# MLP steps of a hybrid decoder trunk: the quarter products set in runs of three, two, four and five

## The chip, the cores and the metric

One Trainium2 chip, one core. The metric is the device time of one execution in microseconds; 3 runs of the kernel before gave 1048.12 to 1048.92 with a median of 1048.6. Matrix products run on TensorE (PE), and ScalarE (ACT) and VectorE (DVE) prepare their operands. SyncE (SP) issues plain DMA loads, and GpSimd (POOL) issues loads that add into their destination ("accumulates").

## The reference

Two layers on 512 rows of width 1024 in float32. Layer 0 mixes by latent attention and layer 1 by gated linear attention; behind each mixer stands the MLP that this case is about:

```python
def sq_relu_mlp(xn, w_up, w_down):          # w_up 1024 x 4096, w_down 4096 x 1024
    hid = jnp.square(jax.nn.relu(xn @ w_up))
    return hid @ w_down

for i in range(DEPTH):                      # DEPTH = 2
    x = x + mixer(rms_norm(x, norm_mix[i]))
    x = x + sq_relu_mlp(rms_norm(x, norm_mlp[i]), w_up[i], w_down[i])
return rms_norm(x, final_norm)
```

## The kernel before

Every float32 operand is split into a high part, which is its rounding to the type that TensorE reads, and a low part, which is the remainder. A product is then three matmuls: high by high, high by low, low by high. For a weight piece, `piece` does the split: ACT writes the high part (`wh`, L110) and then DVE the low part (`wl`, L113), 128 x 1024 elements each, into tiles of four buffers each.

The MLP works in eight blocks of 512 hidden units. In step b (0 to 6) it computes the up product of block b+1 and the down product of block b. Each of the two is a 2 x 2 block product done with seven quarter products in place of eight, in the manner of Strassen and Winograd. So a step has seven `up_product`s (24 matmuls each, 256 columns, L958) and seven `down_product`s (12 matmuls each, 512 columns, L967).

The names: `a11` and `a12` are halves of the up tile A1, `s3` and `a22` of the tile A2, and S1 is a third up tile. `d11`, `d12`, `dS1`, `dS3`, `d22` are down tiles. A2, S1, dS1 and dS3 are sums of two quadrants of the weights, which `fetch` makes with a plain load on SP followed by an accumulate on POOL. `q11` to `q22` are the quarters of the hidden block. Some operands are sums formed on DVE inside the step, among them `d11 = dS1 + d11`, `a11 = S1 + a11` and `q11 = q11 + (q22 - q12)` (with its sign turned later). PSUM has four single banks ("u") for up products and two double banks, "d" and "e", for down products. The output totals S11, S12, SU, S21 and S5 lie in SBUF. S21 and S5 go through a bank: copied in, added onto by the product, and copied out.

Buffers carry over between steps: `after(name)`, called where the tile `name` has had its last use, fetches a tile of the next step into the same room. Which one is a table:

```python
NEXT = {"d11": "dS1", "S1": "S1", "d12": "d11", "A1": "A1", "dS3": "d12", "dS1": "dS3", "A2": "A2", "d22": "d22"}
```

Here the next step's dS1 goes into the room of d11, whose last use is in the fifth product of the step.

Each engine executes its own list of instructions in order. A scheduler makes the lists from the program: it may move an instruction of one product among those of another. The queues of SP and POOL are in order too, and an instruction that waits holds what stands behind it.

## Time and profile before

| | |
|---|---|
| median of 3 runs | 1048.6 us |
| the profiled execution's own time | 1048.94 us |
| its span in the profile | 1047.2 us |
| PE busy | 1038.0 us (99%) |
| DVE, ACT busy | 874.3 us (83%), 699.2 us (67%) |
| granted TensorE clock, mean | 0.998 |

The profiled execution is 0.34 us above the median, and 1.74 us of it lie outside the span. The MLP of layer 0 runs from about 207 to 502 us in the span, that of layer 1 from about 745 us to the end. Busy shares are means over the whole program. What the change is worth is decided inside the MLP steps, on the engine that is never idle there.

### The profile page before, as it was taken

The numbers are of one execution on the slowest core, as the hardware profiler recorded it, in microseconds if no ns is written. First come the engines' busy times: TensorE is split into PE (matmuls) and PEld (weight loads), VectorE is DVE, ScalarE is ACT, GpSimd is POOL, SyncE is SP. The second block draws the span as 40 slices with busy tenths as digits, with TensorE's granted clock in tenths as the row PEclk, the third lists the DMA queues.
The fourth block names the chain that finished last, engine by engine and source line by source line (L and its number), as shares of the span: only waits on it lengthen the run. The fifth ranks groups of instructions, "written<-read, shape, count | busy, mean of one in ns | idle before, by whom it ended". The sixth has DMA issues, their size and how long they took to land.

```text
span 1047.2 us, 15642 instructions
## 1 busy us (share of the span) xinstructions
PE 1038.0 (99%) x5966; PEld 905.1 (86%) x5966; DVE 874.3 (83%) x1340; ACT 699.2 (67%) x1074; POOL 114.6 (11%) x128
## 2 busy tenths in 40 slices
PE   9999999999999999999999999999999999999997
PEld 7788888889999999998888888888888999999995
DVE  7889977989899889898687399469789989989993
ACT  7667754567777777776445475565677777777784
POOL 7400010301101111000000000000010111111000
PEclk9999999999999999999999999999999999999999
DMA  7401235776976887843212222164496697697612
GB/s 230 124 21 41 81 94 148 226 184 159 236 189 151 216 210 161 202 161 121 66 66 81 83 79 67 55 161 152 90 253 153 178 236 171 160 237 185 159 61 81
DMA packets 120492, 149.97 MB, mean 143 GB/s; under 512 B 9344, under 2 KB 86144, under 8 KB 120288
## 3 DMA queue, kind: packets, MB, share of 16 engines
q1 hardware_dynamic: 95920, 117.76, 35.3%
q0 software_dynamic: 22400, 29.36, 17.7%
q10 hardware_dynamic: 2096, 1.84, 0.6%
q8 instruction: 47, 0.77, 0.3%
q14 instruction: 29, 0.24, 0.1%
HBM read 144.49 MB, written 4.19 MB: 142 GB/s over the span
## 4 chain that ended last, share of the span: by engine, by line
PE 90%; DVE 4%; ACT 3%; DMA 2%; issue 1%; SPq 0%; ACTq 0%; DVEq 0%
PE ps L967 26%; PE ps L958 25%; PE ps L118 10%; PE ps L120 10%; PE ps L119 10%; PE ps L1174 2%; PE ps L1429 1%; PE ps L135 1%; PE ps L1209 1%; DVE wl L113 1%; DMA wraw<-in_mla_w_in_dram 1%; PE ps L1556 1%; DVE acc L252 0%; ACT wh L110 0%; DMA xT<-in_x_dram 0%
## 5 line engine op out<-in xcount | busy, mean ns | idle before, releaser
L967 PE MATMUL ps<-wh,set 128*128 128x512 f32 x784 | 253.7, 392 | 0.3 <-ACT set L110 0.3
L110 ACT ACTIVATE wh<-wraw 128x1024 fp32r<-128x1024 f32 x139 | 146.6, 1058 | 97.3 <-PE ps L119 42.0
L113 DVE TENSOR_TENSOR wl<-wraw,wh 128x1024 fp32r<-128x1024 f32 x139 | 170.1, 1224 | 42.7 <-ACT wh L110 41.7
L967 PEld LDWEIGHTS ps<-wh,set 128*128 128x128 f32 x784 | 147.0, 188 | 30.2 <-ACT set L110 0.7
L958 PE MATMUL ps<-T,wh 128*128 128x256 f32 x896 | 156.0, 276 | 0.0
L967 PE MATMUL ps<-wl,set 128*128 128x512 f32 x392 | 152.9, 390 | 0.0
L113 DVE TENSOR_TENSOR wl<-comb,wh 128x1024 fp32r<-128x1024 f32 x112 | 136.7, 1221 | 16.4 <-ACT wh L110 16.4
L958 PEld LDWEIGHTS ps<-T,wh 128*128 128x128 f32 x896 | 137.6, 188 | 2.4
L110 ACT ACTIVATE wh<-comb 128x1024 fp32r<-128x1024 f32 x112 | 118.2, 1056 | 23.4 <-PE ps L958 8.5
L958 PE MATMUL ps<-T,wl 128*128 128x256 f32 x448 | 124.0, 277 | 0.0
L958 PE MATMUL ps<-set,wh 128*128 128x256 f32 x672 | 117.7, 277 | 0.0
L118 PE MATMUL ps<-set,wh 128*128 128x512 f32 x280 | 109.8, 392 | 0.0
L119 PE MATMUL ps<-set,wh 128*128 128x512 f32 x280 | 109.8, 392 | 0.0
L120 PE MATMUL ps<-set,wl 128*128 128x512 f32 x280 | 109.6, 391 | 0.0
L958 PEld LDWEIGHTS ps<-set,wh 128*128 128x128 f32 x672 | 103.8, 188 | 2.4
L958 PE MATMUL ps<-set,wl 128*128 128x256 f32 x336 | 93.2, 277 | 0.0
L967 PEld LDWEIGHTS ps<-wl,set 128*128 128x128 f32 x392 | 73.8, 188 | 13.5
L958 PEld LDWEIGHTS ps<-T,wl 128*128 128x128 f32 x448 | 84.1, 188 | 0.1
L947 POOL DMA_DIRECT2D comb<-in_mlp_w_down_dram x28 | 33.5, 1197 | 304.8 <-DMA comb<-in_mlp_w_down_dram 143.6
L958 PEld LDWEIGHTS ps<-set,wl 128*128 128x128 f32 x336 | 63.1, 188 | 0.0
L120 PEld LDWEIGHTS ps<-set,wl 128*128 128x128 f32 x280 | 52.6, 188 | 11.4 <-DVE wl L113 0.4
L119 PEld LDWEIGHTS ps<-set,wh 128*128 128x128 f32 x280 | 52.6, 188 | 11.1 <-DVE set L750 0.2
(396 smaller groups left out, 2027.0 us busy)
## 6 DMA issues: line engine op xcount, KB each, us to landing
comb<-in_mlp_w_down_dram SPq DMA_DIRECT2D x74, 512.0 KB, 4.9
wraw<-in_mlp_w_up_dram SPq DMA_DIRECT2D x32, 1024.0 KB, 8.2
comb<-in_mlp_w_down_dram POOLq DMA_DIRECT2D x28, 512.0 KB, 7.6
wraw<-in_gla_w_in_dram SPq DMA_DIRECT2D x12, 1024.0 KB, 5.2
comb<-in_mlp_w_up_dram SPq DMA_DIRECT2D x14, 512.0 KB, 4.2
comb<-in_mlp_w_up_dram POOLq DMA_DIRECT2D x14, 512.0 KB, 8.7
wraw<-in_mlp_w_up_dram POOLq DMA_DIRECT2D x14, 512.0 KB, 6.2
wraw<-in_mla_w_o_dram SPq DMA_DIRECT2D x4, 1024.0 KB, 4.9
```

Source lines behind the costliest of these rows:

```text
L110: order(ACT.activation(hi, src, AF.Copy))
L113: lo_eng.tensor_tensor(lo, src, f(hi), ALU.subtract)
L118: PE.matmul(psum, wh, xh, start=start, stop=False)
L119: PE.matmul(psum, wh, xl, start=False, stop=False)
L120: PE.matmul(psum, wl, xh, start=False, stop=stop)
L135: PE.transpose(psum, src, ident[: src.shape[0], : src.shape[0]])
L947: POOL.dma_start(t, q(b, *more), accum_op=ALU.add)
L958: PE.matmul(o, a_, x_, start=start and j == 0 and k == 0 and n == 0, stop=k == KH - 1 and n == 2, skip_group_check=True)
L967: PE.matmul(o, x_, w_, start=start and k == 0 and n == 0, stop=k == 1 and n == 2, skip_group_check=True)
L1174: PE.matmul(p, a, x, start=False, stop=k == 3 and n == 2, skip_group_check=True)
L1209: PE.matmul(o, a, b_, start=False, stop=k == 3 and n == 2, skip_group_check=True)
L1429: PE.matmul(p[:, t - t0], k[:, t * P : (t + 1) * P], moving[:, t], start=True, stop=True)
```

## The change

Step 0 of each layer keeps the old function `step`, with its last two products swapped (`down_21` before `up_t4`). Steps 1 to 6 of each layer use a new function, `step_in_runs`. It has the same fourteen products with the same operands, in the order

D(d11) | U(a11) U(S1) U(a11 + S1) | D(d12) D(d11 + dS1) | U(a12) U(s3) U(22) U(a22) | D(d12 + d11) D(dS3) D(dS1) D(d22)

where U is an up and D a down product. The four last downs and the first one of the next step make five in a row. The total S5 goes through two single "u" banks in place of the double bank "e"; S21 now uses "e". The table of rooms changes: the next dS1 goes into the room of d12, whose last use is now the first of the four last downs, right behind the last use of A2.

```diff
-            opening = b == 0 and nxt is not None
+            opening = nxt is not None
...
-            if b == 0:
-                order = up_t2, down_11, up_t1, down_22, up_22, down_12, up_t3
-            else:
-                order = down_11, up_t2, up_t1, down_22, down_12, up_22, up_t3
-            ends = (up_t4, down_21) if b in (0, NB - 2) else (down_21, up_t4)
-            for product in (*order, down_5, *ends):
+            for product in (up_t2, down_11, up_t1, down_22, up_22, down_12, up_t3, down_5, down_21, up_t4):
                 product()
+
+        def step_in_runs(b, q, r, after):
...
+            def onto(total, a, parts):
+                pair = [bank("u"), bank("u")]
+                cols = [total[:, i * 512 : (i + 1) * 512] for i in range(2)]
+                for p, c in zip(pair, cols):
+                    copied(p, c)
+                down_product(pair, a, parts, False)
+                for p, c in zip(pair, cols):
+                    copied(c, p)
+
+            d = two_banks("d")
+            down_product(d, d11, parts_of_quad(q11), True)
+            e = copied(two_banks("e"), d)
+            DVE.tensor_tensor(d11, ds1, d11, ALU.add)
+            DVE.tensor_tensor(q12, q22, q12, ALU.subtract)
+            DVE.tensor_tensor(q11, q11, q12, ALU.add)
+
+            w, w2, z, y = (bank("u") for _ in range(4))
+            up_product(z, a11, "11", True)
+            copied(y, z)
+            DVE.tensor_tensor(a11, s1, a11, ALU.add)
+            up_product(w, s1, "T1", True)
+            copied(w2, w)
+            after("S1")
+            up_product(z, a11, "T2", False)
+            u = copied(tmp(), z)
+
+            down_product(e, d12, parts_of_quad(q21), False)
+            DVE.tensor_tensor(S11, e, S11, ALU.add)
+            DVE.tensor_tensor(q21, q21, q11, ALU.subtract)
+            down_product(d, d11, parts_of_quad(q11, -1.0), False)
+            e = copied(two_banks("e"), d)
...
+            up_product(z, a22, "T4", False)
+            finish(z, 1, 0, r)
+            after("A2")
+
+            down_product(e, d12, parts_of_quad(q22), False)
+            DVE.tensor_tensor(S12, e, S12, ALU.add)
+            after("d12")
...
+            onto(S5, ds1, parts_of_quad(q22, -1.0))
+            after("dS1")
+            e = copied(two_banks("e"), S21)
+            down_product(e, d22, parts_of_quad(q21, -1.0), False)
+            copied(S21, e)
+            after("d22")
...
-        NEXT = {"d11": "dS1", "S1": "S1", "d12": "d11", "A1": "A1", "dS3": "d12", "dS1": "dS3", "A2": "A2", "d22": "d22"}
+        NEXT = {"S1": "d11", "d11": "S1", "d12": "dS1", "dS3": "d12", "dS1": "dS3", "d22": "d22", "A1": "A1", "A2": "A2"}
...
-            step(b, Q[b % 2], Q[(b + 1) % 2], after)
+            (step_in_runs if b else step)(b, Q[b % 2], Q[(b + 1) % 2], after)
```

Three places in the lists of instructions show what the scheduler made of it, all at the turn from step 2 to step 3 of layer 0.

First, the accumulates on POOL. Before, one round in order is dS1 (`comb_3267`), S1 (`comb_3332`, from the up weights), dS3 (`comb_3469`) and A2 (`wraw_3527`), and then the next dS1:

```order
L947 DMA comb_3267<-in_mlp_w_down_dram 128x2x512
L947 DMA comb_3332<-in_mlp_w_up_dram 128x4x256
L947 DMA comb_3469<-in_mlp_w_down_dram 128x2x512
L937 DMA wraw_3527<-in_mlp_w_up_dram 128x4x256
L947 DMA comb_3657<-in_mlp_w_down_dram 128x2x512
```

After, S1 (`comb_3303`), A2 (`wraw_3439`), dS1 (`comb_3461`), dS3 (`comb_3510`), and then the next S1:

```order
L947 DMA comb_3303<-in_mlp_w_up_dram 128x4x256
L937 DMA wraw_3439<-in_mlp_w_up_dram 128x4x256
L947 DMA comb_3461<-in_mlp_w_down_dram 128x2x512
L947 DMA comb_3510<-in_mlp_w_down_dram 128x2x512
L947 DMA comb_3696<-in_mlp_w_up_dram 128x4x256
```

The accumulate of dS1 stood three ahead of that of A2; it now stands directly behind it, and the list of SP likewise has the plain loads of A1, A2 and dS1 one behind the other.

Second, DVE where the sum with dS1 stands. Before (L1013 is `d11 = dS1 + d11`; L1014 and L1015 make q12 and q11; the L113 rows write low parts):

```order
L113 TENSOR_TENSOR wl_3532<-wraw_3411,wh_3531 128x1024
L1063 TENSOR_TENSOR tmp_3443<-ps_3330,tmp_3441 128x512
L1009 TENSOR_TENSOR wraw_3411<-comb_3332,wraw_3411 128x1024
L859 SCALAR_TENSOR_TENSOR tmp_3445<-tmp_3443,rstd_2203 128x512
L113 TENSOR_TENSOR wl_3565<-comb_3354,wh_3564 128x1024
L1014 TENSOR_TENSOR set_2146<-set_2148,set_2146 128x512
L1013 TENSOR_TENSOR comb_3354<-comb_3267,comb_3354 128x1024
L1015 TENSOR_TENSOR set_2145<-set_2145,set_2146 128x512
```

After (L1105 is that sum, L1107 makes q11, L1112 is `a11 = S1 + a11`; `wl_3565` is the low part of a11, `wl_3595` of S1, and the engine's preceding row L1149 adds a finished product to the total SU):

```order
L113 TENSOR_TENSOR wl_3540<-comb_3230,wh_3539 128x1024
L1149 TENSOR_TENSOR xT<-ps_618_3143,xT 128x1024
L1105 TENSOR_TENSOR comb_3230<-comb_3461,comb_3230 128x1024
L1107 TENSOR_TENSOR set_2145<-set_2145,set_2146 128x512
L113 TENSOR_TENSOR wl_3565<-wraw_3406,wh_3564 128x1024
L113 TENSOR_TENSOR wl_3595<-comb_3303,wh_3594 128x1024
L1112 TENSOR_TENSOR wraw_3406<-comb_3303,wraw_3406 128x1024
```

Before, the low part of a11 and the sum a11 + S1 stood ahead of the sum with dS1; now both stand behind it.

Third, ACT and PE right behind that place. ACT after (L844 turns the sign of q11, `sum` is S5, `xT` is S21, `ps_675_3555<-ps_672_3536` copies bank d into bank e, `wh_3625` is the high part of a11 + S1, `wh_3657` that of d12):

```order
L110 ACTIVATE wh_3564<-wraw_3406 128x1024
L1090 ACTIVATE sum_2157<-ps_3488 128x512
L1090 ACTIVATE sum_2157<-ps_3489 128x512
L110 ACTIVATE wh_3594<-comb_3303 128x1024
L844 ACTIVATE set_2155<-set_2145 128x512
L110 ACTIVATE set_2149<-set_2148 128x512
L1090 ACTIVATE xT<-ps_668_3513 128x1024
L110 ACTIVATE wh_3625<-wraw_3406 128x1024
L110 ACTIVATE set_2151<-set_2146 128x512
L1090 ACTIVATE ps_675_3555<-ps_672_3536 128x1024
L110 ACTIVATE wh_3657<-comb_3484 128x1024
```

PE after, at the end of the product with a11 (`wh_3564`) and the start of the one with S1 (`wh_3594`):

```order
L958 MATMUL ps_3562<-set,wh_3564 128x256 x2
L958 MATMUL ps_3562<-set,wl_3565 128x256
L967 MATMUL ps_675_3555<-wh_3657,set_2153 128x512
L958 MATMUL ps_3560<-T_2332,wh_3594 128x256 x2
L958 MATMUL ps_3560<-T_2332,wl_3595 128x256
```

Before, at the end of the product with a11 (`wh_3531`), PE goes on to the whole product with d11:

```order
L958 MATMUL ps_3530<-set,wh_3531 128x256 x2
L958 MATMUL ps_3530<-set,wl_3532 128x256
L967 MATMUL ps_674_3561<-wh_3564,set_2151 128x512
L967 MATMUL ps_674_3561<-wl_3565,set_2151 128x512
L967 MATMUL ps_674_3561<-wh_3564,set_2152 128x512
```

In the changed kernel a single matmul of the product with d12, which the code has three ups later, stands between the first and the second up of steps 2 to 6. In step 1 two matmuls of it stand there. Its high part `wh_3657` is ten rows behind the high part of a11 on ACT.

More of the change, by code (lines that the diff above doesn't have):

```diff
@@ L962, in down_product @@
             for tt in range(2):
-                o = t[:, tt * 512 : (tt + 1) * 512]
+                o = t[tt] if isinstance(t, list) else t[:, tt * 512 : (tt + 1) * 512]
                 for k in range(2):
@@ L1066, in down_5 @@
             def down_5():
-                onto("e", S5, ds1, parts_of_quad(q22, -1.0), b == 0)
+                onto("e", S5, ds1, parts_of_quad(q22, -1.0), True)
                 after("dS1")
@@ new lines, in step_in_runs, with copied @@
+        def step_in_runs(b, q, r, after):
+            (q11, q12), (q21, q22) = q
+            A1, A2, s1 = W["A1"], W["A2"], W["S1"]
+            a11, a12, s3, a22 = A1[:, :KH], A1[:, KH:], A2[:, :KH], A2[:, KH:]
+            d11, d12, ds1, ds3, d22 = (W[n] for n in ("d11", "d12", "dS1", "dS3", "d22"))
+            def copied(dst, src):
+                ACT.activation(dst, src, AF.Copy)
+                return dst
+            def onto(total, a, parts):
[26 more added lines that the diff above has]
+            e = copied(two_banks("e"), d)
+            DVE.tensor_tensor(d12, d11, d12, ALU.add)
+            after("d11")
+            up_product(y, a12, "21", False)
+            finish(y, 0, 0, r)
+            DVE.tensor_tensor(a12, a11, a12, ALU.add)
+            up_product(z, s3, "T3", False)
+            v = copied(tmp(), z)
+            c = tmp()
+            DVE.tensor_tensor(c, w2, v, ALU.add)
+            finish(c, 1, 1, r)
+            up_product(w, a12, "22", False)
+            c = tmp()
+            DVE.tensor_tensor(c, w, u, ALU.add)
+            finish(c, 0, 1, r)
+            after("A1")
+            up_product(z, a22, "T4", False)
[4 more added lines that the diff above has]
+            after("d12")
+            DVE.tensor_tensor(q22, q22, q11, ALU.subtract)
+            down_product(d, ds3, parts_of_quad(q12), False)
+            DVE.tensor_tensor(SU, d, SU, ALU.add)
+            after("dS3")
+            onto(S5, ds1, parts_of_quad(q22, -1.0))
[4 more added lines that the diff above has]
+            after("d22")
@@ L1129, in at_the_end @@
                 DVE.tensor_tensor(S12, S12, S5, ALU.add)
+            if name == "dS1":
                 t = comb(home[name])
```

## The prediction

> **What bounds the kernel now.** I read the page first, then the busy times of one MLP step, then the chain of work that ended last inside it, and at last the instructions and transfers next to the places that the change moves. From the page:

> ```profile
> span 1047.2 us, 15642 instructions
> ...
> PE 1038.0 (99%) x5966; PEld 905.1 (86%) x5966; DVE 874.3 (83%) x1340; ACT 699.2 (67%) x1074; POOL 114.6 (11%) x128
> ...
> PEclk9999999999999999999999999999999999999999
> ...
> PE 90%; DVE 4%; ACT 3%; DMA 2%; issue 1%; SPq 0%; ACTq 0%; DVEq 0%
> ```

> TensorE is the bound, and its clock was granted nearly in full throughout. A mean over the span does not tell what a step allows, so here is one step of layer 0 (busy time and count of each engine):

> ```profile
> core 0: us, PE busy (x) PEld busy (x) DVE busy (x) ACT busy (x) POOL busy (x), PEclk, DMA share, GB/s
> 326.00:364.40 38.40, 38.40 (x254) 35.00 (x253) 34.77 (x39) 28.42 (x36) 6.26 (x5) 1.00 0.76 192
> ```

> TensorE has no idle time in these 38.40 us. VectorE has 3.6 us to spare, ScalarE 10.0. The chain of waits through the same step (start, us, what) holds PE alone:

> ```profile
> 326.01 2.75 PE ps L967 x12
> 328.77 2.77 PE ps L958 x24
> 331.53 5.47 PE ps L967 x24
> 337.01 5.49 PE ps L958 x48
> 342.49 5.47 PE ps L967 x24
> ...
> 358.93 5.49 PE ps L958 x48
> 364.41 2.75 PE ps L967 x12
> ```

> An up (L958, 24 matmuls) alone takes 2.77, two in a row 5.49, so the second takes 2.72. A down (L967, 12 matmuls) alone takes 2.75, two 5.47, again 2.72 for the second. So a change from one kind to the other costs 0.05 or 0.03 us, 0.04 in the mean, and that is all that a better order can win here. In return any wait that PE meets in a step is lost in full.

> **Part by part: fewer changes of kind.** By the lists of instructions, PE changes kind 126 times in both MLPs before and 98 times after. 28 x 0.04 is a gain of 1.1 us. It would be 1.0 more without the stray matmuls in twelve steps, which add two changes each.

> **The stray matmuls and the sum with dS1.** This is the term that decides. In steps 2 to 6 the first matmul of the d12 product stands right behind the a11 product, and PE takes it in order. It needs the high part of d12, which is the last row of a list on ACT; that list passes L844, which needs q11 from DVE, and the high part of a11 + S1, which needs L1112 from DVE. Both of these stand behind L1105 on DVE, which waits until the accumulate of dS1 has landed. The nearest rows of VectorE (start, us), where the sum with dS1 is L1013, and of ScalarE are:

> ```profile
> 321.65 1.22 DVE L1013 TENSOR_TENSOR comb<-comb,comb 128x1024 f32<-128x1024 f32 x1
> 322.79 0.69 DVE L1015 TENSOR_TENSOR set<-set,set 128x512 f32<-128x512 f32 x1
> 323.39 1.22 DVE L113 TENSOR_TENSOR wl<-wraw,wh 128x1024 fp32r<-128x1024 f32 x1
> ```

> ```profile
> 323.21 1.06 ACT L110 ACTIVATE wh<-comb 128x1024 fp32r<-128x1024 f32 x1 [0.29 <-PE ps L958]
> 324.18 0.61 ACT L844 ACTIVATE set<-set 128x512 fp32r<-128x512 f32 x1
> ...
> 328.58 0.63 ACT L110 ACTIVATE set<-set 128x512 fp32r<-128x512 f32 x1 [0.57 <-PE ps L967]
> 329.12 1.01 ACT L976 ACTIVATE ps<-ps 128x1024 f32<-128x1024 f32 x1
> 330.06 1.04 ACT L110 ACTIVATE wh<-wraw 128x1024 fp32r<-128x1024 f32 x1
> ```

> L1013 waits for nothing now: it starts before L1015 has to, with no idle time shown. From start to start a 1024 row takes 1.14 on DVE (321.65 to 322.79), a 512 row 0.60; on ACT 0.97 for a high part, 0.54 for a 512 row, 0.94 for the copy of a bank. After a late landing DVE does L1105 1.14, q11 0.60, low parts of a11 and S1 2 x 1.14, L1112 1.22: 5.2 us. Then ACT does the high part 0.97, the 512 row 0.54, the copy 0.94 and the high part of d12 1.06: 3.5. Sum 8.7, and with the hand-over 8.8 from the landing to the stray matmul.

> When does PE want it? Count from the start t of the four ups. The high part of a22 (the last use of A2) stands on ACT behind L844 and the copy of d into e, which waits for the down just ended: 0.54 + 0.94 + 1.04, then the low part 1.22 on DVE, so A2's room is free at t + 3.8. Four ups take 10.9 (2 x 5.49 less one change), five downs 13.7 (5.47 + 5.47 + 2.72), so the next a11 product starts at t + 24.6 and the stray matmul is due at t + 27.4. The landing would have to be at t + 18.6, which is 14.8 us behind the release of A2.

> When does dS1 land? On SP its load is queued behind those of A1 and A2, and on POOL its accumulate behind that of A2, which waits for A2's load. The rows: the loads and accumulates on the page (KB each, median us to landing), the accumulates' queue, a single load and accumulate, and the issues on POOL and SP with their starts:

> ```profile
> wraw<-in_mlp_w_up_dram SPq DMA_DIRECT2D x32, 1024.0 KB, 8.2
> comb<-in_mlp_w_down_dram POOLq DMA_DIRECT2D x28, 512.0 KB, 7.6
> comb<-in_mlp_w_up_dram POOLq DMA_DIRECT2D x14, 512.0 KB, 8.7
> wraw<-in_mlp_w_up_dram POOLq DMA_DIRECT2D x14, 512.0 KB, 6.2
> ...
> q0 software_dynamic: 22400, 29.36, 17.7%
> ```

> ```profile
> wraw<-in_mlp_w_up_dram SPq DMA_DIRECT2D x1, 1024.0 KB, 5.6
> ...
> comb<-in_mlp_w_up_dram POOLq DMA_DIRECT2D x1, 512.0 KB, 10.7
> ```

> ```profile
> 276.55 0.37 SPq L140 DMA_DIRECT2D wraw<-in_mlp_w_up_dram  x1
> ...
> 258.28 1.19 POOL L947 DMA_DIRECT2D comb<-in_mlp_w_down_dram  x1 [14.36 <-DVE set L113]
> 262.06 1.31 POOL L947 DMA_DIRECT2D comb<-in_mlp_w_up_dram  x1 [2.59 <-DVE set L1069]
> 282.80 1.32 POOL L937 DMA_DIRECT2D wraw<-in_mlp_w_up_dram  x1 [4.38 <-DVE wl L113]
> ```

> A2's load takes between 5.6 (the load issued at 276.55) and the median 8.2: 6.9. It landed at 282.15 there, and POOL's accumulate followed at 282.80: 0.6. Two accumulates in flight: from below 6.2 for A2's, which has always run alone, plus the time that one keeps 16 engines, 17.7% of 1047.2 over 56, 3.3: 9.5. From above the pair issued at 258.28 and 262.06, with plain loads beside it as here: its second landed 10.7 after issue, at 272.76, 14.5 behind the first issue. Middle 12.0. So dS1 lands 6.9 + 0.6 + 12.0 = 19.5 behind the release, 4.7 too late. PE has no room in which to win that back, so each of five turns in each of two layers costs 4.7: 47 us. Of the 4.7, PE waits 1.7 for the low part of a11 (ready 1.14 + 0.60 + 1.22 behind the landing at t + 23.3, wanted at t + 24.6) and 3.0 at the stray matmul. The bounds are 5.6 + 0.6 + 9.5 = 15.7 (0.9 late, 9 us) and 8.2 + 0.6 + 14.5 = 23.3 (8.5 late, 85 us). Three fifths of the way to either end, 24 and 70, is what I take into the range, since all extremes together are unlikely.

> [...]

> **Step 1.** Its two stray matmuls wait for the low part of d12 on DVE, with no late landing ahead. Between nothing and the time of one product, 2.8; I take half, 1.4 in each layer, 2.8 in all.

> **What I cost at nothing.** The copies of S5 in four pieces instead of two add 1 us of ACT per step, which has 10.0 idle; without that cover the turn would cost up to 1.0 more. DVE does the same 39 instructions. Of the other fetches S1, A2 and dS3, which need an accumulate, have nine products or more until use, over 24 us, and the plain loads d11, d12, d22 and A1 six or more, over 16 us. Swapping the last two products of step 0 leaves no wait, and the last product of step 6 is the same down onto S21.

> **Sum.** 47 + 2.8 - 1.1 = 48.7 over the profiled execution of 1048.94, which is 0.34 above the median of the three runs. On the median: 1048.6 + 48.7 = 1097.3, say 1097.

> **The rivals.** *In time.* The two loads of A1 and A2 stream as one, the accumulates overlap, and dS1 lands within 14.8. The point of decision is the time of A2's load plus the pair: at 5.6 + 0.6 + 8.6 or less no turn waits. For it speaks the 3.3 us that an accumulate really occupies; against it every observed pair. Then only the fewer changes and step 1 are left, between -1.1 and +1.7: 1047.5 to 1050.3. That case alone can end faster or the same. Chance 0.09.

> *Later still.* All the transfers of the turn (A1, A2, dS1, d12, dS3, d22 and two accumulates within some 16 us) hold each other up as at the upper bound: 85 + 1.7, about 1135. For it speaks a DMA share of 0.76 now as a mean over the step. Chance 0.10.

> *The clock falls.* PE stands still 3.0 us before each stray matmul; if its clock then dropped to half for the length of one product, 2.7 us would be added ten times: 1124. [...] Chance 0.06.

> The forecast has 0.75. Its own range, 24 + 1.7 to 70 + 1.7 above the median, is 1074 to 1120. The range that I give reaches on to the clock's case, 1074 to 1126, and leaves out the first two rivals. A measurement here can tell a difference of about 0.2%, 2.1 us; a gain as large would need nearly twice the changes that were removed. So faster has 0.02, the same 0.06, and slower 0.92.

> **What would show it.** In the profile after: L1105 on DVE with idle time before it, released by a DMA into comb; a single L967 matmul behind each first up of steps 2 to 6 with PE idle before it, released by ACT wh L110; steps of some 43 us in place of 38.4; other products at 2.72. I am wrong if L1105 does not wait, if PE stays without gaps, or if it waits somewhere else (in the five downs, or at the low parts of the four ups).

## The result and the profile after

The changed kernel takes 1114.5 us (median of four runs, 1112.0 to 1120.0) against 1048.5 for the kernel before on the same chip: a ratio of 1.0637 with a 95% interval of 1.0596 to 1.0678. The forecast was 1097 in a range of 1074 to 1126. The profiled execution took 1113.3, 64.4 more than that of before, and the rows below are from it.

The head of the page and its chain of work, after:

```profile
span 1111.6 us, 15717 instructions
...
PE 1057.6 (95%) x5966; PEld 921.1 (83%) x5966; DVE 875.1 (79%) x1340; ACT 696.6 (63%) x1098; POOL 113.9 (10%) x128
...
PEclk9999999999999999999999999999999999999999
...
PE 71%; DMA 10%; DVE 9%; ACT 6%; issue 4%; POOL 0%; DVEq 0%; SPq 0%; ACTq 0%; POOLq 0%
```

PE executes the same 5966 matmuls, but is busy for 1057.6 us in place of 1038.0, and the span has grown by 64.4: so 44.8 us are new idle time, and for 19.6 more PE was busy with the same matmuls. The line of the clock cannot show the second part, because its tenths are means over 28 us. In the chain a transfer, DMA, now stands second with 10%, before 2%.

What PE and DVE wait for (us in total, times, longest), the rows of PE first:

```profile
PE ps L967 <- ACT wh L110: 26.7, 10, 3.0
PE ps L958 <- DVE wl L113: 16.1, 10, 2.4
PE ps L967 <- DVE wl L113: 1.7, 2, 0.8
...
DVE comb L1105 <- DMA comb<-in_mlp_w_down_dram: 55.7, 10, 6.4
```

Ten times, once in each turn between steps, DVE waits at L1105 for the accumulate of dS1; ten times PE waits, in the mean 1.6 us for the low part of a11 and 2.7 for the high part of d12 at the stray matmul. The two waits of 0.8 are those of step 1. The chain of waits through the turn from step 2 to step 3 in layer 0 (start, us, what):

```profile
318.06 0.77 POOL wraw L937
318.84 0.50 issue
319.34 11.69 DMA comb<-in_mlp_w_down_dram
...
331.12 0.10 DVE comb L1105
...
332.26 0.68 DVE set L1107
332.94 1.21 DVE wl L113 x2
...
335.13 1.23 DVE wraw L1112
...
337.35 0.61 ACT set L110
337.96 0.91 ACT ps L1090
338.87 0.98 ACT wh L110
339.86 0.04 issue
339.90 0.50 PE ps L967
340.39 6.62 PE ps L958 x44
```

This is the path that the forecast gave: A2's accumulate is issued on POOL, dS1's behind it lands after 11.69 us at 331.03, then DVE makes the sum, q11, two low parts and a11 + S1, ACT three rows, and PE runs the one stray matmul at 339.90, 8.9 us behind the landing.

The loads of A1 and A2 on SP that open it (start of the first, us from there to the end of the last issue):

```profile
308.54 3.68 SPq L140 DMA_DIRECT2D wraw<-in_mlp_w_up_dram  x2
```

A2's load is the second of the two, issued 311.86, at the release of its room. So dS1 landed 19.2 us behind the release, where the forecast had 19.5 and 14.8 were allowed. Over the ten turns it is 18.9 to 20.5, with a mean of 19.7. The accumulates on the page (KB each, median us to landing), where before had 7.6 and 6.2 for these:

```profile
comb<-in_mlp_w_down_dram POOLq DMA_DIRECT2D x28, 512.0 KB, 8.0
...
wraw<-in_mlp_w_up_dram POOLq DMA_DIRECT2D x14, 512.0 KB, 10.0
```

What a turn costs is seen best in the stretch from the start of the product with a11 to the end of the product with a11 + S1. Ten such stretches of the changed kernel, of which the first, the fifth and the sum are shown (start and end, length, busy time and count of each engine, granted clock):

```profile
287.73:302.83 15.10, 10.68 (x75) 10.23 (x73) 13.93 (x17) 8.50 (x11) 0.00 (x0) 0.89 0.21 66
...
467.06:481.45 14.39, 10.50 (x75) 9.96 (x74) 14.36 (x17) 8.52 (x11) 0.00 (x0) 0.88 0.18 46
...
sum 148.32, PE 105.54 PEld 100.69 DVE 139.13 ACT 86.27 POOL 0.00; mean PE 10.55 PEld 10.07 DVE 13.91 ACT 8.63 POOL 0.00
```

The same stretch without any wait is in the first experiment below (dS1 in its old room):

```profile
287.92:296.37 8.45, 8.45 (x74) 8.40 (x73) 8.38 (x10) 5.59 (x7) 1.31 (x1) 1.00 0.64 127
```

Ten turns cost 148.3 - 84.5 = 63.8 us, nearly the whole of the 64.4. And PE's busy time in a turn is 10.55 in place of 8.45: that is the part that the forecast did not count. The granted clock is 0.88 or 0.89 in all ten. One turn in three stretches shows where:

```profile
293.30:296.72 3.42, 1.35 (x10) 1.31 (x11) 3.42 (x5) 3.42 (x5) 0.00 (x0) 1.00 0.37 137
296.72:300.13 3.41, 3.41 (x18) 3.41 (x18) 3.27 (x4) 0.13 (x2) 0.00 (x0) 0.50 0.00 0
300.13:303.54 3.41, 3.41 (x29) 3.28 (x28) 2.38 (x2) 2.08 (x3) 0.00 (x0) 1.00 0.54 155
```

PE stood still for 2.1 of 3.42 us ahead of the stray matmul; then the clock was half for 3.41 us, in which 18 matmuls ran in place of 29, and then full again.

### The profile page after: what moved, and what is told of

It is laid out like the page before. It is cut to its first block, busy times and chain, and to the rows that moved or that the text cites. A ratio compares the mean times of both kernels' runs of the same rounds, so it can differ in the third digit from the quotient of the medians.

```text
span 1111.6 us, 15717 instructions
## 1 busy us (share of the span) xinstructions
PE 1057.6 (95%) x5966; PEld 921.1 (83%) x5966; DVE 875.1 (79%) x1340; ACT 696.6 (63%) x1098; POOL 113.9 (10%) x128
## 3 DMA queue, kind: packets, MB, share of 16 engines
q0 software_dynamic: 22400, 29.36, 16.4%
q10 hardware_dynamic: 2096, 1.84, 0.5%
## 4 chain that ended last, share of the span: by engine, by line
PE 71%; DMA 10%; DVE 9%; ACT 6%; issue 4%; POOL 0%; DVEq 0%; SPq 0%; ACTq 0%; POOLq 0%
PE ps L958 16%; PE ps L967 14%; PE ps L118 10%; PE ps L120 10%; PE ps L119 9%; DMA comb<-in_mlp_w_down_dram 8%; DVE wl L113 4%; ACT wh L110 2%; PE ps L1280 2%; PE ps L1245 2%; PE ps L1500 1%; PE ps L135 1%; DVE wraw L1112 1%; PE ps L421 1%; ACT ps L1090 1%
## 5 line engine op out<-in xcount | busy, mean ns | idle before, releaser
L967 PE MATMUL ps<-wh,set 128*128 128x512 f32 x784 | 250.5, 393 | 27.0 <-ACT wh L110 26.7
L110 ACT ACTIVATE wh<-wraw 128x1024 fp32r<-128x1024 f32 x139 | 146.2, 1055 | 138.3 <-PE ps L958 51.9
L113 DVE TENSOR_TENSOR wl<-wraw,wh 128x1024 fp32r<-128x1024 f32 x139 | 169.9, 1222 | 49.4 <-ACT wh L110 49.1
L967 PEld LDWEIGHTS ps<-wh,set 128*128 128x128 f32 x784 | 147.2, 188 | 58.9 <-ACT wh L110 28.8
L958 PE MATMUL ps<-T,wh 128*128 128x256 f32 x896 | 166.6, 288 | 0.0
L967 PE MATMUL ps<-wl,set 128*128 128x512 f32 x392 | 153.1, 390 | 1.7 <-DVE wl L113 1.7
L113 DVE TENSOR_TENSOR wl<-comb,wh 128x1024 fp32r<-128x1024 f32 x112 | 136.6, 1220 | 21.2 <-ACT wh L110 21.2
L958 PEld LDWEIGHTS ps<-T,wh 128*128 128x128 f32 x896 | 146.5, 200 | 1.3
L110 ACT ACTIVATE wh<-comb 128x1024 fp32r<-128x1024 f32 x112 | 117.2, 1054 | 35.0 <-issue 14.1
L958 PE MATMUL ps<-T,wl 128*128 128x256 f32 x448 | 128.8, 288 | 0.0
L958 PE MATMUL ps<-set,wh 128*128 128x256 f32 x672 | 120.7, 281 | 0.0
L958 PE MATMUL ps<-set,wl 128*128 128x256 f32 x336 | 95.4, 284 | 16.1 <-DVE wl L113 16.1
L958 PEld LDWEIGHTS ps<-set,wh 128*128 128x128 f32 x672 | 105.9, 192 | 2.3
L958 PEld LDWEIGHTS ps<-T,wl 128*128 128x128 f32 x448 | 89.6, 200 | 0.1
L967 PEld LDWEIGHTS ps<-wl,set 128*128 128x128 f32 x392 | 73.7, 188 | 16.5 <-DVE wl L113 2.3
L958 PEld LDWEIGHTS ps<-set,wl 128*128 128x128 f32 x336 | 64.5, 192 | 18.1 <-DVE wl L113 18.1
L947 POOL DMA_DIRECT2D comb<-in_mlp_w_up_dram x14 | 18.3, 1305 | 516.8 <-PE ps L135 218.1
L844 ACT ACTIVATE set<-set 128x512 fp32r<-128x512 f32 x42 | 26.4, 630 | 69.9 <-DVE set L1107 45.4
## 6 DMA issues: line engine op xcount, KB each, us to landing
comb<-in_mlp_w_down_dram SPq DMA_DIRECT2D x74, 512.0 KB, 5.4
wraw<-in_mlp_w_up_dram SPq DMA_DIRECT2D x32, 1024.0 KB, 5.6
comb<-in_mlp_w_down_dram POOLq DMA_DIRECT2D x28, 512.0 KB, 8.0
wraw<-in_gla_w_in_dram SPq DMA_DIRECT2D x12, 1024.0 KB, 5.2
comb<-in_mlp_w_up_dram SPq DMA_DIRECT2D x14, 512.0 KB, 3.7
comb<-in_mlp_w_up_dram POOLq DMA_DIRECT2D x14, 512.0 KB, 6.0
wraw<-in_mlp_w_up_dram POOLq DMA_DIRECT2D x14, 512.0 KB, 10.0
wraw<-in_mla_w_o_dram SPq DMA_DIRECT2D x4, 1024.0 KB, 4.9
```

The source lines that it names most:

```text
L110: order(ACT.activation(hi, src, AF.Copy))
L113: lo_eng.tensor_tensor(lo, src, f(hi), ALU.subtract)
L844: ACT.activation(hi, src, AF.Copy, scale=sign)
L947: POOL.dma_start(t, q(b, *more), accum_op=ALU.add)
L958: PE.matmul(o, a_, x_, start=start and j == 0 and k == 0 and n == 0, stop=k == KH - 1 and n == 2, skip_group_check=True)
L967: PE.matmul(o, x_, w_, start=start and k == 0 and n == 0, stop=k == 1 and n == 2, skip_group_check=True)
```

## The experiments

All times are medians, and ratios are to the kernel before on the same chip. In these texts "in order" means that PE's matmuls of steps 1 to 6 keep the order of the program, so that no matmul stands stray.

**The order and the table apart.** The change has a new order of products and a new table of rooms. The first experiment keeps the new order and takes the old table; the second keeps the old order and takes the new one.

```diff
-        NEXT = {"S1": "d11", "d11": "S1", "d12": "dS1", "dS3": "d12", "dS1": "dS3", "d22": "d22", "A1": "A1", "A2": "A2"}
+        NEXT = {"d11": "dS1", "S1": "S1", "d12": "d11", "A1": "A1", "dS3": "d12", "dS1": "dS3", "A2": "A2", "d22": "d22"}
```

> The changed kernel with the old table of rooms: the next dS1 goes into the room of d11 (free after the second pair of downs, 5 products earlier than the room of d12 that is used five downs before the turn). Order of products and stray matmuls as in the changed kernel. Late landing (the forecast's theory): L1105 does not wait, the ten turns cost nothing, TensorE's clock stays full; what is left is the gain of fewer changes (-1.1) and the two stray matmuls of step 1 (1.2 each): 1048.5 + 1.4 = 1050, between 1048 and 1052. Rival, bunching (five downs in a row ask more of DVE and ACT than 13.7 us hold, whenever dS1 lands): the waits stay, over 1090. Rival, the stray matmul by itself: PE still waits about 3 us at each stray matmul, 1075 or more.

> The kernel before, its order of products untouched, with the new table of rooms alone: the next dS1 goes into the room of d12, whose last use is here the seventh product of the step or so. Late landing: the room is free some ten products ahead of the next sum with dS1 and A2's accumulate comes behind, so nothing waits: 1048.5 within 1 us. It takes the new order and the new table together. Rival, the table by itself (this room is too late in any order): L1013 waits in ten turns, 1065 or more.

Measured: the new order with the old table 1049.2 (1.0012, interval 1.0003 to 1.0021), the old order with the new table 1048.2 (1.0001, 0.9991 to 1.0010). In the first, DVE has no wait at L1105, and the median of the accumulates of down tiles on the page falls to

```profile
comb<-in_mlp_w_down_dram POOLq DMA_DIRECT2D x28, 512.0 KB, 5.9
```

from 8.0 in the changed kernel. So neither half costs anything that matters; only together do they cost 65. The late room hurts in the new order because there the sum with dS1 stands on DVE ahead of the low part of a11, which PE needs for the second product of the next step.

**The stray matmuls.** PE in order, with the new table and with the old one:

```diff
+        in_order = lambda i: tc.keep_in_program_order(i) if W.get("runs") else i
...
-                        PE.matmul(o, a_, x_, start=start and j == 0 and k == 0 and n == 0, stop=k == KH - 1 and n == 2, skip_group_check=True)
+                        in_order(PE.matmul(o, a_, x_, start=start and j == 0 and k == 0 and n == 0, stop=k == KH - 1 and n == 2, skip_group_check=True))
```

The matmul at L967 is wrapped in the same way.

> The changed kernel with its late room for dS1, but the matmuls of steps 1 to 6 kept in the order of the code on PE, so that no matmul of the d12 product stands behind the first up. Late landing: L1105 waits as long as before, PE waits some 1.6 us for the low part of a11 and then some 2 us for the high part of a11 + S1 at the third up, no longer 2.7 at the stray matmul; step 1 has no wait. Ten turns of 3.6 us less 2.1 for fewer changes: 1082 if the clock stays full, 1099 if it falls for one window of 3.4 us per turn. Rival, the stray matmul by itself: all waits gone, 1046 to 1049.

> The changed order with the old table of rooms and PE in the order of the code: no late dS1, no stray matmul. Late landing: no PE wait in steps 1 to 6, and PE changes kind 126 - 98 + 24 = 52 times less than before, at 0.04 us: -2.1 us, 1046.4, ratio 0.998. Rival, bunching: over 1085. Rival, the price of a change of kind does not add up (it is a start-up of each product that another wait hides): 1048.5, ratio 1.000.

Measured: with the new table 1095.1 (1.0454, 1.0436 to 1.0472), with the old one 1047.0 (0.9988, 0.9979 to 0.9997). The second is the only version here that is faster than the kernel before, by 1.1 us or 0.12%. That is about half of what was forecast for fewer changes of kind, 1.1 plus 1.0 without the stray matmuls. PE has no waits in its steps and is busy for 2.0 us less than in the kernel before (1038.0):

```profile
span 1045.4 us, 15714 instructions
...
PE 1036.0 (99%) x5966; PEld 904.3 (86%) x5966; DVE 873.8 (84%) x1340; ACT 698.0 (67%) x1098; POOL 114.5 (11%) x128
```

Against the first experiment (1049.2) the strays of all twelve steps cost 2.3 without a late landing. With the new table, order alone wins 19 us and 48 stay. PE still waits ten times for the low part of a11, and in five turns at the third up:

```profile
PE ps L958 <- DVE wl L113: 22.8, 10, 3.1
PE ps L958 <- ACT ps L1090: 7.2, 5, 2.0
```

The expectation named the high part of a11 + S1 for the second wait. The row shows another: the third up adds onto the bank of the first, and ACT must copy that bank out first (`copied(y, z)`). In one turn of layer 0 the high part of a11 + S1 was written by 335.80 and its low part by 337.06, but the copy, which stands on ACT behind the high part of d12, took from 339.06 to 339.64. The third up began at 339.69. So this wait too hangs on the landing, through ACT's list.

**Where the landing is lost.** Two kernels leave the late room and the stray matmuls as they are. In one A2's accumulate is left out; in the other A2's load and accumulate are queued behind those of dS1.

```diff
-                if c:
-                    POOL.dma_start(W[name][:, :KH], up_quadrant(b, 0, 0), accum_op=ALU.add)
```

> The changed kernel with the accumulate of A2 left out: A2 stays a plain quadrant, so part of the up sums is not computed. All else, the late room of dS1 and the stray matmuls included, stays. Theory (dS1 is late because its accumulate stands behind that of A2): the landing of dS1 moves forward by the time it spent behind A2's, from 19.5 us behind the release to some 15 to 16, against the 14.8 that are allowed, so that a turn waits 0.5 to 1.5 us in place of 4.3 and the clock has no reason to drop: 1048.5 + 10 x 0.5..1.5 + 2.5 of step 1 - 1.1, some 1055 to 1065, and a mean clock of 0.998. Rival (the loads alone bring dS1 too late, and the accumulate of A2 has no part in it): waits and time stay, 1110 to 1115.

```diff
             finish(z, 1, 0, r)
-            after("A2")
...
             after("d12")
+            after("A2")
...
+                if b and new == "A2":
+                    on_sp, on_pool = W["issued dS1"]
+                    with tc.issue_after(on_sp.ins), tc.issue_after(on_pool.ins):
+                        return fetch(b + 1, new)
```

> The changed kernel with the late room of dS1 and its stray matmuls, in which A2's load on SP and accumulate on POOL are queued behind those of dS1 in place of ahead of them; the lists of PE, DVE and ACT are the changed kernel's row for row. dS1's load then starts when the room of d12 is free, 1.7 us behind the release of A2, takes 5.2 to 6.1, and its accumulate follows 0.6 later and takes 6.0 to 7.8 without A2's ahead of it: landing 13.5 to 16.2 behind the release in place of 19.5, where 14.8 are allowed. Theory (the place in the two queues is what makes dS1 late, not the room): between nothing and 1.4 us late per turn, 1049 to 1064. Rival (the late room alone is too late, whatever stands ahead in the queues): as with A2's accumulate left out, 1081, or worse, up to 1114.

Measured: without A2's accumulate 1080.9 (1.0316, 1.0286 to 1.0345), above the 1055 to 1065 expected; with the queues turned round 1065.6 (1.0161, 1.0139 to 1.0184), at the upper end of what was expected. The waits, first without the accumulate, then with the queues turned round:

```profile
PE ps L967 <- ACT wh L110: 21.7, 10, 2.7
...
DVE comb L1105 <- DMA comb<-in_mlp_w_down_dram: 28.8, 10, 3.5
```

```profile
PE ps L967 <- ACT wh L110: 13.6, 10, 2.6
...
DVE comb L1105 <- DMA comb<-in_mlp_w_down_dram: 20.8, 10, 3.3
```

DVE's wait per turn falls from 5.6 to 2.9 and to 2.1, and the wait for the low part of a11 is gone in both. One row of the chain of waits in each, in the same order, from issue to landing (the first from the turn from step 2 to step 3 of layer 0, the second from step 5 to step 6):

```profile
318.04 7.75 DMA comb<-in_mlp_w_down_dram
```

```profile
435.13 9.89 DMA comb<-in_mlp_w_down_dram
```

The place behind A2 in the two queues is thus worth 49 of the 66 us, the half-clock stretches that go with the waits included (ten in the turns of the changed kernel, one in those of the kernel with the queues turned round). It is not all of it.

What the place does can be read from the issues and landings of the ten turns in each kernel. dS1's plain load is issued 5.51 us behind the start of the four ups in every one of the thirty turns, whether A2's load stands ahead of it on SP or behind, and its accumulate follows the load's landing by 0.6 to 0.7 us. So neither waits noticeably in its queue. What differs is how long they take. In the changed kernel the load takes 5.5 us in the mean and the accumulate 11.9 (10.6 to 12.8). With the queues turned round these are 4.2 and 9.7 (9.0 to 10.9), though A2's accumulate still runs behind dS1's: 1.3 us of each turn come from the load and 2.2 from the accumulate. Without A2's accumulate they are 6.3 and 8.4 (6.7 to 9.4), with no accumulate ahead and that of dS3 behind.

The landings are 19.7, 16.2 and 17.0 us behind the release of A2's room, in the same order, where 14.8 are allowed. Without A2's accumulate 15 to 16 were expected, so the time fell less than expected. The rival "the room alone is too late" keeps a part: 17 us are left with the best place in the queues. No run moved the sum with dS1 behind the low parts of a11 and S1 on DVE, where it stood before the change; whether that alone would have hidden the late landing is open.

**The small banks.** The fastest version (PE in order, old table), but with S5 through the double bank e:

```diff
-                pair = [bank("u"), bank("u")]
...
-                down_product(pair, a, parts, False)
-                for p, c in zip(pair, cols):
-                    copied(c, p)
+                t = copied(two_banks("e"), total)
+                down_product(t, a, parts, False)
+                copied(total, t)
```

> The kernel with PE kept in the program's order and the old table of rooms (1047.0 us), with S5 through the double bank e in place of two small banks. S21 uses e right behind it and the sum with d12 right ahead of it. Theory (the two small banks are needed, since e must be copied out, copied in and read by PE between two downs that follow each other directly): PE waits in the five downs of steps 1 to 6 ahead of the products with dS1 and d22, for at least one copy out and one copy in each time, 2 x 0.94 us less nothing that covers it: between 1.9 and 3.2 us per step in twelve steps, 23 to 38 us, and up to 1.7 us more for each half-clock stretch that such a wait brings with it (at most 20): 1070 to 1105. Rival (the scheduler finds other work for PE or the copies of e are early enough, and the small banks make no difference): 1046 to 1049.

Measured: 1106.8 (1.0557, 1.0539 to 1.0574), just above the range. The waits and the first of them in layer 0 (start, us, in brackets the idle time before):

```profile
PE ps L967 <- ACT ps L1090: 32.2, 12, 3.0
```

```profile
326.43 0.50 PE L967 MATMUL ps<-wh,set 128*128 128x512 f32 x1 [3.04 <-ACT ps L1090]
```

The part of the change that sends S5 through two small banks is needed: without it the five downs stop once in each of twelve steps, and the clock falls behind some of the stops (0.50 from 327.52 to 330.93, behind the one shown; its mean is 0.985).

**What the half clock costs.** The first run puts idle work (22 matmuls whose result is overwritten) into the wait for a11's low part, with PE in order and the new table:

```diff
+            for k in range(22 if b > 1 else 0):
+                in_order(PE.matmul(z[:, :TH], quad["T1"][k % KH][:, 0][:, :P], quad["T1"][k % KH][:, 0], start=True, stop=True, skip_group_check=True))
             up_product(z, a11, "11", True)
```

> The kernel with the late room of dS1 and PE in the program's order (1095.1 us), with 22 matmuls of 256 columns more on PE ahead of the product with a11 in steps 2 to 6, whose result is overwritten. They take 22 x 0.113 = 2.5 us, about as long as PE waits there for the low part of a11, so that PE does idle work in place of standing still. Theory (a wait of over about half of a 3.4 us stretch makes the clock drop to half for the next 3.4 us, which costs 1.7 us each time; there were seven such stretches): the time that dS1 is late stays, the half-clock stretches at the first up go, and the mean clock rises from 0.988 to 0.995 or more: 1095 - 5..7 x 1.7, some 1083 to 1087. If the matmuls were longer than the wait, up to 3 us more. Rival (the clock in the records costs no time, or drops for another reason than the waits): 1094 to 1098.

Measured: 1095.9 (1.0454, 1.0433 to 1.0475), the same as without the idle work, at a mean clock of 0.998 in place of 0.988. The expectation was wrong and its rival right, in that kernel. Two turns without the idle work show why, one at full clock and one with two stretches at half:

```profile
328.99:342.56 13.57, 8.77 (x74) 8.36 (x72) 13.08 (x15) 8.42 (x11) 0.00 (x0) 1.00 0.20 55
372.59:386.60 14.01, 11.35 (x74) 11.15 (x72) 13.97 (x16) 8.51 (x11) 0.00 (x0) 0.76 0.15 45
```

With the half clock PE is busy 2.6 us longer, and the turn is 0.4 longer. The third up has to wait for ACT's copy of its bank either way, so slower matmuls ahead of it only shorten that wait: it is 1.7 us in the first of these turns and none in the second. Does the same hold in the changed kernel, where the stray matmul waits and nothing does behind it? The next two runs wrote the stray matmul by hand between the first and the second up, the second of them with 26 idle matmuls ahead of it:

```diff
+            d12_product = down_matmuls(e, d12, parts_of_quad(q21), False)
+            if b > 1:
+                next(d12_product)
             up_product(w, s1, "T1", True)
```

> The kernel with the late room of dS1 and PE in the program's order (1095.1 us), with the first matmul of the product with d12 written by hand between the first and the second up of steps 2 to 6, where the changed kernel has it; the other engines keep the lists of the changed kernel. Step 1 has no stray matmuls. Theory (one matmul in the wrong place is all that separates the two): the changed kernel again less step 1, 1114.5 - 2.5 = 1112, clock 0.985. Rival (the order of the rest of PE's list matters too): it stays near 1095.

> The kernel before this one with 26 matmuls of 256 columns ahead of the stray matmul in steps 2 to 6, whose result is overwritten: 26 x 0.113 = 2.9 us, about the 3.1 that PE stands still there. When the stray matmul runs is set by the chain from the landing, so idle work costs nothing. Theory (the half-clock stretch right behind the stray matmul, over the second up, costs 1.6 to 1.75 us in each of ten turns because no wait follows that it could be hidden in): the mean clock goes to 0.995 or more, and 1112 - 16..17 = 1095 to 1096; where the wait was shorter than 2.9 (two turns) up to 1 us more each. Rival (the clock costs nothing, as in the run with idle work ahead of the first up, where it rose to 0.998 and the time stayed): 1110 to 1114.

Measured: 1085.3 (1.0357, 1.0339 to 1.0376) and 1101.5 (1.0508, 1.0492 to 1.0523). Neither theory saw this. With the product written earlier, ACT made the operand of d12 ahead of that of a11 + S1, so PE stood idle ahead of the stray matmul for only 0.6 us in eight turns and not at all in two, and over half of the 30 us of idle work was added time. So they say nothing on the clock. They do say that the stray matmul by itself costs little where its operand is made early: dS1 lands as late as in the changed kernel (19.9 us behind the release in the mean, against 19.7), and yet the first of these kernels is 10 us faster than the one without a stray matmul (1095.1). The last pair brings ACT's and DVE's lists back to those of the changed kernel in these steps:

```diff
+            w_s1 = piece(s1, KH, 256, at=AT_UP)
+            w_a11 = piece(a11, KH, 256, at=AT_UP)
+            d12_product = down_matmuls(e, piece(d12, 2, 512), parts_of_quad(q21), False)
```

> The run before with the stray matmul written by hand was no clean one: ACT and DVE took the operand of the product with d12 ahead of that of a11 + S1, so the stray matmul hardly waited. Here the three operands are made in the order S1, a11 + S1, d12, and the lists of ACT, DVE, POOL and SP are those of the changed kernel row for row; PE's list differs in step 1 alone, which has no stray matmuls. Theory (the stray matmul and what follows from it is all that separates the changed kernel from the one with PE in order, 1095): 1114.5 - 2.5 for step 1 = 1112, clock 0.984 to 0.986, ten half-clock stretches. Rival: 1095.

> The kernel before this one with idle work on PE in steps 2 to 6: 3 matmuls of 256 columns ahead of the product with a11 and 26 ahead of the stray matmul, 2.9 us of the 3.1 that PE stands still there; the results are overwritten, and the other engines' lists keep their order in these steps. The chain from the landing to the stray matmul, and so the wait, stays. Theory (each half-clock stretch over the second up is lost in full, 1.6 to 1.75 us, since nothing waits behind it): where the clock stays full a turn is that much shorter; with eight to ten such turns 1112 - 13..17 = 1095 to 1099, mean clock 0.993 or more. Rival (the half clock costs no time): 1110 to 1114 at the higher clock.

Measured: 1111.5 (1.0616, 1.0580 to 1.0651), the changed kernel less step 1 as expected; and with idle work 1110.3 (1.0596, 1.0568 to 1.0623), where 1095 to 1099 was expected. Against the 1085.3 above, the order in which ACT and DVE make the operands is worth 26 us, at nearly the same late landing (20.2 us behind the release). The total does not show the clock's price. The turns do. Here is one of the first kernel, then two of the second, with the length and the granted clock:

```profile
331.21:346.19 14.98, 10.50 (x74) 10.00 (x73) 13.79 (x17) 8.51 (x11) 0.00 (x0) 0.89 0.19 64
```

```profile
287.60:301.16 13.56, 11.99 (x101) 11.61 (x100) 13.53 (x17) 8.52 (x11) 0.00 (x0) 1.00 0.14 43
331.33:347.52 16.19, 13.41 (x102) 13.16 (x100) 14.90 (x17) 8.51 (x11) 0.00 (x0) 0.89 0.22 64
```

The first two have the same waits to within 0.06 us (1.79 and 1.85 at the low part of a11, 3.25 and 3.28 to the stray matmul, from start to start): with the clock full the turn is 1.4 shorter. Six of the ten turns kept the clock. In the other four it fell earlier, behind the wait for a11's low part, and then the idle work started late and stood in the way, as in the third row. That, and the three idle matmuls ahead of each turn, took back what the six gained.

The queue experiments hold the same comparison without any idle work, since their clock fell only in one or two turns (its mean is 0.996 in both). First without A2's accumulate, then with the queues turned round, a turn with a fall and one without:

```profile
370.30:383.26 12.96, 10.21 (x74) 9.92 (x73) 11.80 (x14) 7.27 (x9) 0.00 (x0) 0.87 0.23 71
927.98:939.10 11.12, 8.73 (x75) 8.47 (x73) 11.09 (x14) 6.92 (x9) 0.00 (x0) 1.00 0.15 50
```

```profile
327.32:340.23 12.91, 10.34 (x74) 10.09 (x73) 11.63 (x14) 7.08 (x9) 0.00 (x0) 0.87 0.29 85
449.23:459.72 10.49, 8.75 (x75) 8.50 (x73) 10.46 (x13) 6.45 (x8) 0.00 (x0) 1.00 0.31 76
```

The lengths differ by 1.84 and 2.42, the idle times (length less PE's busy time) by 0.36 and 0.83, so the half clock costs 1.5 and 1.6. In three kernels, then, a fall with no wait behind it costs 1.4 to 1.6 us, in single turns set side by side; no total shows it.

## Why the prediction came out as it did

**The place and the chain: right.** L1105 waits for the DMA, a single L967 matmul stands behind the first up with PE idle ahead of it, released by ACT wh, and nothing waits in the five downs or the four ups. The landing came 19.2 us behind the release in the turn shown, against 19.5. The middle value for two accumulates in flight, 12.0 from the issue of A2's to the landing of dS1's, measured 331.03 - 318.06 = 13.0 in that turn; a shorter A2 load (5.6, forecast 6.9) made up for it. In the mean of the ten turns these are 13.2 and 5.8. That the landing came out so close is therefore partly luck: two errors of over 1 us cancel.

**The wait per turn: right within a tenth.** Forecast 1.7 and 3.0; idle time measured 1.6 and 2.7. The forecast's 47 us for ten turns stand against 42.8 us of idle time in them (148.3 - 105.5).

**The clock: the term that the sum left out.** The time lies within the range, but 17 us above the sum, and here is most of it. The sum took every matmul at its full speed: "other products at 2.72". Instead the second up took 3.8 to 4.4 us in eight of the ten turns. The forecast had this as a rival at 0.06, as the alternative to its sum, at 2.7 us for each turn. That was the author's estimate, and no run shows a fall at this price: it came on top of the sum, in all ten turns, at 1.4 to 1.6 by the comparisons above. Eight turns lose it in full: 8 x 1.5 = 12. In the other two (the row at 467.06 is one) the fall came already in the product with a11, which took 1.6 longer, and the wait at the stray matmul was shorter by about as much, 1.45 in place of 2.98. So of the 63.8 us of the turns 42.8 are idle time and 21.0 longer busy time: 12 in the eight turns, 3 in the two, which the shorter wait gave back, and some 6 in the matmuls next to each wait, which are not separated further. The rival was given little weight. In the kernel before no wait of PE was longer than 1.2 us, so its trace was no evidence on a change whose own forecast put 3.0 us of idle time into every turn.

**Step 1 and the changes of kind: small terms, both put too high.** All strays of a kernel without late landings cost 2.3 (1049.2 against 1047.0), forecast 2.8 for step 1 and 1.0 for the changes. The gain of a clean order is 1.1 in the median, forecast 2.1. The spans of the two profiled executions differ by 1.8, but these ran on different chips.

**What was costed at nothing** held: PE waits nowhere in the steps for the four copies of S5, and the old table with the new order has no waits there but the two of step 1, 0.8 us each, and none with PE in order.

## What to carry to other kernels

When a tile moves to a room that comes free later, follow its load and its accumulate through every queue that they stand in: here 49 of 66 us were two places in two queues, and turning them round needed no other change. Look not only at when a transfer is issued but at what runs beside it. Then follow the operands that hang on it through the lists of the other engines: their order alone was worth 26 us. A wait on TensorE had a second price in the clock here, 1.4 to 1.6 us for a fall with no other wait behind it; where one followed, 2.6 us more of busy PE made the turn only 0.4 longer. So look for it per stretch, since a mean hides it. Where two halves of a change cost nothing alone, run them alone and together before blaming either.

## What the runs showed of the hardware that was not expected

The length of the gap alone does not decide. In the in-order kernel with the new table PE stood still for 3.1 us up to 332.49 and the clock stayed full, 1.00 from 328.99 to 342.56. With the changed kernel's trace cut into stretches of 3.41 us from 6.6 to 1105.7 us, the ten ahead of a fall had PE idle for 60% to 87% of the time, and no other more than 49% (1.66 us, from 952.08 to 955.50). No run was made to test this.

Accumulates of 512 KB took very different times from issue to landing. Those of the down tiles have a median of 5.9 us in the kernel with the old room. That of dS1 took 6.7 to 9.4 in the late room without A2's accumulate, 9.0 to 10.9 with A2's queued behind it, and 10.6 to 12.8 with A2's ahead, ten turns each. What of this is the other accumulate and what the plain loads of the turn was not separated.
